# Layer 3 of a four-layer trunk: split q and gate projections, low parts formed on GpSimd, and a new order of norms and gates around the scans

## Chip, core and metric

The kernel runs on one core of a Trainium2 chip. Five engines share that core's work: TensorE (PE; its weight loads are listed apart as PEld), VectorE (DVE), ScalarE (ACT), GpSimd (POOL) and SyncE (SP), which issues most DMAs. Each engine takes its instructions in a fixed order and waits on semaphores for the others. The metric is the device time of one execution in microseconds, the median of several runs.

## What is computed

The reference is a trunk of four layers over 256 latent tokens and 256 context tokens of width 1024, batch 1, all in float32. Layer i takes one mixer and then an MLP. The change touches the mixer of layer 3, a bidirectional gated DeltaNet with 8 key heads and 16 value heads of width 128, in chunks of 64 tokens:

```python
q, k, v = jnp.split(jax.nn.silu(_centred_dwconv(qkv, conv_w)), ...)
q = jnp.repeat(_l2_norm(heads(q)), 2, axis=1) * 128 ** -0.5
k = jnp.repeat(_l2_norm(heads(k)), 2, axis=1)
...
t_inv = lax.linalg.triangular_solve(lmat, eye, lower=True, unit_diagonal=True)
...
def step(s, inp):
    v_new = u_c - w_c @ s
    o = q_c @ s + a_c @ v_new
    s = s * d_c[..., None, None] + jnp.swapaxes(k_c, -1, -2) @ v_new
...
y = (_merge_heads(_rms_norm(o_f + _flip(o_b), norm_g)) * jax.nn.silu(z)) @ w_out
```

z is the gate, another projection of the same input. Layer 3 is the last, so queries, gates and outputs are needed for the latent tokens alone; keys and values are needed for all 512.

## The kernel before

One Python program writes the instructions, and a tile framework orders them on each engine by its own estimate and inserts the semaphores; pools of a fixed number of buffers set how far work may run ahead.

**Projections.** A float32 weight block of 128x1024 is fetched by SP (`raw`), cast on ACT to a high part (`whi`, line 279), and DVE subtracts to get the low part (`wlo`, line 280). `mm3` then makes three products per 128 rows of input (lines 296 to 298: low x high, high x high, high x low). Four raw buffers and four pairs of parts are shared by all blocks; `weights()` keeps two blocks ahead of the one in use. For q and z alone there is another way: `gdn_whole` (line 1542) multiplies the raw float32 block with a float32 copy `u` of the input, eight times 128x256, which the PE runs as two passes each; ACT and DVE have nothing to do for those blocks.

**Products and solves** (`gdn_products`). Keys, queries, values and gates are projected; q, k and v go through a five-tap convolution (`conv`: one ACT scaling and four DVE operations on line 1392, which read PSUM). The value heads are done in two groups of eight. For each group `gdn_solve` makes the decay matrices (lines 1410 to 1421), then runs a loop of 31 steps that inverts 32x32 triangles with two DVE operations a step (lines 1446 and 1448, all operands in SBUF), then joins the blocks by small matmuls (lines 1462 and 1478) and writes the result to DRAM (`uc`, line 1483). Between its steps the jobs of `GDN_JOBS` are started, at the rates of `GDN_PLAN`: a value head (`v`, spilled to DRAM by POOL on line 1591) or a gate head (`z`, spilled on line 1598). POOL otherwise clears buffers and spills the decay matrices (`at`, line 1421).

**Scans** (`gdn_scans`). Four chains c0 to c3, each of eight dependent steps, read the spilled data back. Lanes of jobs are advanced side by side: c0, c1 and the two gate heads that were left; then c2, c3 and a lane with the query norms `n` and the finishing of groups 0 and 1 (`f0`, `f1`); then `f2 f3`. A finish normalises a group's output, gates it, transposes it (line 1718) and multiplies it with four weight blocks `gdn_out` (96 products a group, lines 296 to 298 with `yh` and `yl`), and adds to the residual (line 579).

```python
GDN_LANES = ("c0", "c1", "z"), ("c2", "c3", "n f0 f1"), ("f2 f3",)
GDN_RATES = (1, 1, 0.5), (1, 1, 1.5), (1,)
```

Of the kernel before, what the change touches and what calls it, by code (L numbers as in the profile page):

```python
# [12 lines left out]
F32 = mybir.dt.float32  # L13
# [3 lines left out]
ALU = mybir.AluOpType  # L17
# [4 lines left out]
S = 256  # L22
# [4 lines left out]
KT = D // 128  # L27
# [2 lines left out]
DIFF_AHEAD = 3  # L30
GLA_ROWS = dict(qk=4, la=3, e=9, kb=2, at=1, ob=2)
GLA_STEPS = 2, 1, 1
GDN_LANES = ("c0", "c1", "z"), ("c2", "c3", "n f0 f1"), ("f2 f3",)
GDN_RATES = (1, 1, 0.5), (1, 1, 1.5), (1,)
GDN_ROWS2 = 4, 4, 3, 6, 3, 4
GDN_BANKS = dict(accs=3, st=3, ax=2)
GDN_PLAN = (0, 0.5, 0.4), (0, 0.6, 0.75)
GDN_JOBS = "q0 k1 q1 v v v z z z v v v z z v v z v z v v z z v v z z z z v v z v".split()
TABLES = "natural_log_exp_and_others"
GDN_ROWS = dict(y=3, x=2, v=2, side=3)  # L40
ADA_SUMS = 1
# [116 lines left out]
class Trunk:  # L158
# [100 lines left out]
    def load(self, name, *at):  # L259

        src = self.I[name]
        for j in at:
            src = src[j]
        if name in ("gdn_q", "gdn_z"):
            return self.whole(src)
        last = name == "mla_in" and at[0] in (4, 5) or name in ("mla_out", "diff_out", "gla_out") and at[0] >= 4 or name == "w2" and at[1] >= 4 and at[2] == 3
        return self.halved(self.tail if last else self.wsplit, src)

    def whole(self, src):
        raw = self.wraw.tile([128, 1024], F32, name="raw")  # L270
        self.nc.sync.dma_start(raw[:, :src.shape[-1]], src)
        return raw

    def halved(self, pool, src, n=""):

        nc, width = self.nc, src.shape[-1]
        raw = self.whole(src)
        hi, lo = (pool.tile([128, 1024], F32R, name=m + n) for m in ("whi", "wlo"))
        nc.scalar.copy(hi[:, :width], raw[:, :width])  # L279
        nc.vector.tensor_sub(lo[:, :width], raw[:, :width], hi[:, :width].bitcast(F32))  # L280
        return hi, lo

    def blocks(self):
# [466 lines left out]

    gdn_jobs = GDN_JOBS

# [732 lines left out]
    def gdn_keys(self, grp, key, given=()):  # L1485

        given = list(given)
        n = T2 if key else S
        for j in range(4):
            h = 4 * grp + j  # L1490
            ps = given.pop(0) if given else next(self.proj([("gdn_k", h)])) if key else self.gdn_whole("gdn_q", h)
            y = self.conv(ps, (8 if key else 0) + h, n // S)
            if key:
                self.kT[h] = self.ktp.tile([128, T2], F32, name="kT")
            self.stored(self.silu, self.kT[h] if key else self.qT(h), y, n // S)
            yield
# [42 lines left out]
        self.rsqrt(flat(w), flat(x))  # L1539
        nc.vector.tensor_scalar_mul(self.qnorm, w, -0.5 * 128 ** -0.5)  # L1540

    def gdn_whole(self, name, h):

        w, ps = self.weights(name, h), self.acc()
        for k in range(KT):
            self.nc.tensor.matmul(ps[:, :S], lhsT=w[:, 128 * k:128 * k + 128], rhs=self.u[:, k], start=k == 0, stop=k == KT - 1)  # L1546
        return ps

    def gdn_kk(self, grp):
        nc = self.nc  # L1550
        self.kk = {}
# [40 lines left out]

    def gdn_gate(self, h):
        nc, I = self.nc, self.I
        zp = self.gdn_whole("gdn_z", h)
        sz = self.zs.tile([128, S], F32, name="s")
        self.silu(sz, zp[:, :S])
        nc.gpsimd.dma_start(self.spill[f"z{h // 4}"][:, h % 4], sz)
# [140 lines left out]
    def gdn_open(self, ctx):  # L1739

        nc = self.nc
        pool = self.opener(ctx)
        self.kept, self.ktp = pool("gdn", 1, side="right"), pool("gdnk", 8, side="right")
        side = self.opener(self.uctx)
        self.u = side("gdnu", 1, side="right").tile([128, KT, S], F32, name="u")
        self.zs = side("gdnzs", 2, side="right")
        self.zheads = iter(range(16))
        dram = pool("gdnd", 1, space=bass.MemoryType.DRAM)
        self.gnorm = self.kept.tile([128, 1], F32, name="gnorm")
        nc.vector.tensor_scalar_mul(self.gnorm, self.col("gdn_norm"), -0.5)  # L1750
        self.qnorm = self.kept.tile([128, 2, 8], F32, name="qn")
        self.pick = self.kept.tile([128, 15], F32, name="pick")
        nc.vector.memset(self.pick, 0.0)
        nc.vector.memset(self.pick[:, 7:8], 1.0)
        self.kT, self.o = {}, {}
        self.spill = {"residual": dram.tile([128, KT, S], F32, name="residual")}
        for a in range(4):
            self.spill[f"v{a}"] = dram.tile([128, 4, 4, 128], F32, name=f"v{a}")
            self.spill[f"z{a}"] = dram.tile([128, 4, S], F32, name=f"z{a}")
        for g in range(2):  # L1760
            for p in range(2):
                self.spill[f"uc{g}{p}"] = dram.tile([128, 32, 64], F32, name=f"uc{g}{p}")
                self.spill[f"at{g}{p}"] = dram.tile([128, 2, 512], F32, name=f"at{g}{p}")

    def gdn_products(self):

        nc = self.nc
        with ExitStack() as ctx:
            pool = self.opener(ctx)
            self.open_acc(pool)  # L1770
            rings = {n: pool("gdn" + n, b) for n, b in GDN_ROWS.items()}
            rings["t512"] = self.tmp
            self.rows = lambda n="t512", w=T2: rings[n].tile([128, w], F32, name=n)
            self.srow = lambda: self.rows("side")

            nc.gpsimd.dma_start(self.spill["residual"], self.z[:, :, :S])
            self.lpool, self.x4, self.outer = pool("gdnl", 1), pool("gdnx", 1), pool("gdnt", 1)
            self.once = pool("gdnc", 1)
            self.gdn_tables(self.once)
            first = list(self.proj([("gdn_ba",)] + [("gdn_k", h) for h in range(3)], outer=[64] + [128] * 3))  # L1780
            ba = self.srow()
            self.stored(lambda o, x: nc.scalar.copy(o, x), ba[0:64], first[0][0:64], 2)

            def some(gen, n=None):
                for _ in islice(gen, n):
                    pass

            done, values = set(), iter(range(16))

            def jobs():  # L1790
                for job in self.gdn_jobs:
                    if job[0] in "kq":
                        yield from self.gdn_keys(int(job[1]), job[0] == "k")
                    elif job == "v":
                        yield self.gdn_value(next(values))
                    else:
                        yield self.gdn_gate(next(self.zheads))
                    done.add(job)

            def until(job):  # L1800
                while job not in done:
                    next(main)

            for k in range(KT):
                nc.vector.tensor_tensor(self.u[:, k], *(x[:, k, :S].bitcast(F32) for x in (self.uh, self.ul)), op=ALU.add)
            self.gdn_gates(self.once, self.srow, ba)
            some(self.gdn_keys(0, True, first[1:]))
            main = jobs()
            for grp, n in enumerate(GDN_PLAN):
                until(f"q{grp}")  # L1810
                self.gdn_kk(grp)
                self.gdn_kq(grp)
                if grp == 0:
                    self.gdn_decays(self.kept)
                self.gdn_key_norms(grp)
                due = 0
                for step, _ in enumerate(self.gdn_solve(grp)):
                    due += n[(step >= 8) + (step >= 39)]
                    while due >= 1:
                        some(main, 1)  # L1820
                        due -= 1
            some(main)

    def gdn_scans(self):
        nc = self.nc
        with ExitStack() as ctx:
            pool = self.opener(ctx)
# [27 lines left out]
                            if next(gens[j][0], left) is left:  # L1855
                                left.remove(j)

            def gates():
                for h in self.zheads:
                    self.gdn_gate(h)  # L1860
                    yield

            kinds = dict(z=gates, c=self.gdn_chain, f=self.gdn_finish, n=self.gdn_query_norms)
            lane = lambda jobs: chain.from_iterable(kinds[j[0]](*map(int, j[1:])) for j in jobs.split())
            for n, lanes in enumerate(GDN_LANES):
                if n == 1:
                    self.tables()
                    self.uctx.close()
                    right = lambda *a: pool(*a, side="right")
                    self.zp, self.yp = right("gdnz", 1), right("gdny", 1)  # L1870
                    self.open_ln(right, S)
                    nc.sync.dma_start(self.z[:, :, :S], self.spill["residual"])
                together(*((lane(jobs), rate) for jobs, rate in zip(lanes, GDN_RATES[n])))
            self.ln_finish(*LAT)

# [66 lines left out]
```

## Time and profile before

| what | value |
|---|---|
| median of 3 runs | 2735.97 us (2731.73 to 2740.79) |
| the profiled execution, its own time | 2734.95 us |
| its span, first to last instruction | 2733.2 us |
| busy: PE, DVE, ACT, POOL | 96%, 73%, 46%, 2% of the span |
| mean granted TensorE clock | 0.985 of full speed |

Layer 3's mixer lies between about 2000 and 2520 us of the span; before it are layers 0 to 2, after it the last MLP. A matmul's end is modelled, so a PE that is shown busy is not at its peak; the distance from one start to the next tells what a matmul costs. Idle time of an engine counts only where something else waits for it.

### The profile page before, as it was taken

How to read it: one execution, taken by the hardware profiler on the slowest of the kernel's cores; microseconds unless marked ns; L12 is line 12 of the kernel's file. 1: busy time of each engine (PE TensorE's matmuls, PEld its weight loads, DVE VectorE, ACT ScalarE, POOL GpSimd, SP SyncE). 2: the span in 40 equal slices, each digit the busy share in tenths (PEclk: the TensorE clock that was granted, in tenths of full speed). 3: DMA queues.
4: the chain of work that ended last, by engine and by line, in shares of the span. 5: the costliest groups of instructions: out<-in, count | busy, mean ns of one | idle time of the engine just before them, and what ended most of it. 6: DMA issues, size and time to landing. Idle time of an engine off the chain costs nothing. (4 is left out here: it accounts for less than half of the span.)

```text
span 2733.2 us, 40942 instructions
## 1 busy us (share of the span) xinstructions
PE 2630.0 (96%) x15728; PEld 2137.2 (78%) x15728; DVE 2007.7 (73%) x3796; ACT 1251.6 (46%) x2413; POOL 46.2 (2%) x71
## 2 busy tenths in 40 slices
PE   7999999999999999999999999999999998997998
PEld 5666888888866687888888897888887776667997
DVE  3577898775667798775745489876689996679666
ACT  3555453234556653333445553332464545445544
POOL 0000000000000000000000000000000111000000
PEclk9999999999999999999999999999999998999999
DMA  6533246553221137554221127654323445304453
GB/s 237 169 121 111 68 155 207 185 185 118 65 64 54 47 100 225 191 184 131 73 70 62 55 70 226 195 181 153 104 85 105 160 151 157 90 28 139 155 183 111
DMA packets 125535, 353.25 MB, mean 129 GB/s; under 512 B 37499, under 2 KB 41339, under 8 KB 124828
## 3 DMA queue, kind: packets, MB, share of 16 engines
q1 hardware_dynamic: 121804, 337.00, 38.8%
q0 software_dynamic: 3536, 13.63, 1.4%
q8 instruction: 124, 2.03, 0.3%
q14 instruction: 71, 0.58, 0.1%
HBM read 335.91 MB, written 14.68 MB: 128 GB/s over the span
## 5 line engine op out<-in xcount | busy, mean ns | idle before, releaser
L279 ACT CAST whi<-raw 128x1024 fp32r<-128x1024 f32 (+2 forms) x403 | 410.7, 1024 | 681.6 <-PE acc L297 244.9
L280 DVE TENSOR_TENSOR wlo<-raw,whi 128x1024 fp32r<-128x1024 f32 (+2 forms) x403 | 477.9, 1189 | 209.5 <-ACT whi L279 197.5
L296 PE MATMUL pj<-ul,whi 128*128 128x512 f32 (+1 forms) x1072 | 395.1, 369 | 0.1
L297 PE MATMUL pj<-uh,whi 128*128 128x512 f32 (+1 forms) x1072 | 385.2, 359 | 0.0
L298 PE MATMUL pj<-uh,wlo 128*128 128x512 f32 (+1 forms) x1072 | 383.8, 358 | 0.7 <-DVE wlo L280 0.5
L452 DVE SCALAR_TENSOR_TENSOR acc<-raw,s,acc 128x1024 f32<-128x1024 f32 x252 | 317.2, 1280 | 34.9 <-DMA raw<-in_ada 31.6
L296 PE MATMUL acc<-ul,whi 128*128 128x512 f32 (+3 forms) x888 | 312.5, 352 | 17.6 <-DVE ul L568 10.7
L297 PE MATMUL acc<-uh,whi 128*128 128x512 f32 (+3 forms) x888 | 309.8, 349 | 0.0
L298 PE MATMUL acc<-uh,wlo 128*128 128x512 f32 (+3 forms) x888 | 308.5, 348 | 0.1
L296 PEld LDWEIGHTS pj<-ul,whi 128*128 128x128 f32 x1072 | 204.0, 190 | 36.4 <-issue 6.1
L298 PEld LDWEIGHTS pj<-uh,wlo 128*128 128x128 f32 x1072 | 203.5, 190 | 34.6 <-issue 5.4
L297 PEld LDWEIGHTS pj<-uh,whi 128*128 128x128 f32 x1072 | 203.8, 190 | 29.4 <-issue 5.2
L296 PEld LDWEIGHTS acc<-ul,whi 128*128 128x128 f32 (+2 forms) x888 | 168.6, 190 | 42.3 <-DVE ul L568 12.7
L296 PE MATMUL pj<-hl,whi 128*128 128x512 f32 (+1 forms) x560 | 196.5, 351 | 1.7 <-DVE hl L635 1.3
L297 PE MATMUL acc<-hh,whi 128*128 128x512 f32 (+1 forms) x560 | 195.4, 349 | 0.0
L297 PE MATMUL pj<-hh,whi 128*128 128x512 f32 (+1 forms) x560 | 194.8, 348 | 0.0
L296 PE MATMUL acc<-hl,whi 128*128 128x512 f32 (+1 forms) x560 | 194.8, 348 | 0.0
L298 PE MATMUL acc<-hh,wlo 128*128 128x512 f32 (+1 forms) x560 | 194.7, 348 | 0.0
L298 PE MATMUL pj<-hh,wlo 128*128 128x512 f32 (+1 forms) x560 | 194.2, 347 | 0.0
L298 PEld LDWEIGHTS acc<-uh,wlo 128*128 128x128 f32 (+2 forms) x888 | 168.4, 190 | 21.8 <-issue 1.0
L297 PEld LDWEIGHTS acc<-uh,whi 128*128 128x128 f32 (+2 forms) x888 | 168.5, 190 | 20.9 <-issue 1.2
L634 ACT CAST hh<-t 128x512 fp32r<-128x512 f32 (+1 forms) x128 | 72.2, 567 | 129.7 <-DVE t L633 129.3
(463 smaller groups left out, 4887.2 us busy)
## 6 DMA issues: line engine op xcount, KB each, us to landing
raw<-in_w SPq DMA_DIRECT2D x256, 512.0 KB, 4.2
raw<-in_ada SPq DMA_DIRECT2D x192, 512.0 KB, 4.7
raw<-in_diff_qk SPq DMA_DIRECT2D x16, 512.0 KB, 3.4
raw<-in_gdn_v SPq DMA_DIRECT2D x16, 512.0 KB, 4.0
raw<-in_gdn_z SPq DMA_DIRECT2D x16, 512.0 KB, 4.0
raw<-in_gdn_out SPq DMA_DIRECT2D x16, 512.0 KB, 3.9
raw<-in_mla_in SPq DMA_DIRECT2D x9, 512.0 KB, 7.0
raw<-in_mla_qb SPq DMA_DIRECT2D x12, 384.0 KB, 3.8
```

The lines of the kernel that those rows point to most:

```text
L279: nc.scalar.copy(hi[:, :width], raw[:, :width])
L280: nc.vector.tensor_sub(lo[:, :width], raw[:, :width], hi[:, :width].bitcast(F32))
L296: mm(ps, lhsT=ah, rhs=bl, start=start, stop=False)
L297: mm(ps, lhsT=ah, rhs=bh, start=False, stop=False)
L298: mm(ps, lhsT=al, rhs=bh, start=False, stop=stop)
L452: nc.vector.scalar_tensor_tensor(acc[r], w, self.s[:, k, r:r + 1], acc[r], op0=ALU.mult, op1=ALU.add)
L634: nc.scalar.copy(hh[:, f, :t], r[:, :t])
```

## The change

Gate and query projections become split products like the others, the low parts of the layer's five weights are made by POOL, `u` goes, all sixteen gate heads become jobs of the product stage, the query norms move beside c0 and c1, and `f0 f1` have their lane beside c2 and c3 to themselves. With no gate left in the scans, the pools of the finishes open, and the residual is fetched back, ahead of the first lanes.

```diff
-GDN_LANES = ("c0", "c1", "z"), ("c2", "c3", "n f0 f1"), ("f2 f3",)
-GDN_RATES = (1, 1, 0.5), (1, 1, 1.5), (1,)
+GDN_LANES = ("c0", "c1", "n"), ("c2", "c3", "f0 f1"), ("f2 f3",)
+GDN_RATES = (1, 1, 1), (1, 1, 1.5), (1,)
...
-GDN_JOBS = "q0 k1 q1 v v v z z z v v v z z v v z v z v v z z v v z z z z v v z v".split()
+GDN_JOBS = "q0 k1 q1 v v v z z z v v v z z v v z v z v v z z v v z z z z v v z v z z".split()
+
+LOW_APART = "gdn_k", "gdn_q", "gdn_v", "gdn_z", "gdn_out"
...
-        if name in ("gdn_q", "gdn_z"):
-            return self.whole(src)
...
-        return self.halved(self.tail if last else self.wsplit, src)
+        return self.halved(self.tail if last else self.wsplit, src, low=self.nc.gpsimd if name in LOW_APART else None)
...
-        nc.vector.tensor_sub(lo[:, :width], raw[:, :width], hi[:, :width].bitcast(F32))
+        (low or nc.vector).tensor_sub(lo[:, :width], raw[:, :width], hi[:, :width].bitcast(F32))
...
-            ps = given.pop(0) if given else next(self.proj([("gdn_k", h)])) if key else self.gdn_whole("gdn_q", h)
+            ps = given.pop(0) if given else next(self.proj([("gdn_k", h)])) if key else next(self.proj([("gdn_q", h)], S))
...
-        zp = self.gdn_whole("gdn_z", h)
+        (zp,) = self.proj([("gdn_z", h)], S)
...
-            for k in range(KT):
-                nc.vector.tensor_tensor(self.u[:, k], *(x[:, k, :S].bitcast(F32) for x in (self.uh, self.ul)), op=ALU.add)
...
+            self.tables()
+            self.uctx.close()
+            right = lambda *a: pool(*a, side="right")
+            self.zp, self.yp = right("gdnz", 1), right("gdny", 1)
+            self.open_ln(right, S)
+            nc.sync.dma_start(self.z[:, :, :S], self.spill["residual"])
             for n, lanes in enumerate(GDN_LANES):
-                if n == 1:
-                    self.tables()
-                    self.uctx.close()
...
                 together(*((lane(jobs), rate) for jobs, rate in zip(lanes, GDN_RATES[n])))
```

On DVE, in the loop of the first group's solve, before (`outer` and `xc` are the loop's own tiles, `y` a convolution):

```order
L1448 TENSOR_TENSOR xc<-xc,outer 128x2x26x6
L280 TENSOR_TENSOR wlo<-raw,whi 128x1024
L1446 TENSOR_TENSOR outer<-xb,xc 128x350
L1392 SCALAR_TENSOR_TENSOR y<-acc,cols,y 128x254
L1448 TENSOR_TENSOR xc<-xc,outer 128x2x25x7
```

and at the same place now:

```order
L1448 TENSOR_TENSOR xc<-xc,outer 128x2x26x6
L1392 SCALAR_TENSOR_TENSOR y<-acc,cols,y 128x254
L1446 TENSOR_TENSOR outer<-xb,xc 128x350
L1392 SCALAR_TENSOR_TENSOR y<-acc,cols,y 128x255
L1448 TENSOR_TENSOR xc<-xc,outer 128x2x25x7
```

The subtraction is gone from between the loop's steps; steps and convolutions still take turns.

On POOL, from the decay matrices of the first group on, the order is now (the numbered names are the DRAM tiles of the spills):

```order
L280 TENSOR_TENSOR wlo<-raw,whi 128x1024 x12
L1421 DMA at_17228<-side 128x512 x2
L280 TENSOR_TENSOR wlo<-raw,whi 128x1024
L1421 DMA at_17230<-side 128x512
L280 TENSOR_TENSOR wlo<-raw,whi 128x1024 x2
L1421 DMA at_17230<-side 128x512
L280 TENSOR_TENSOR wlo<-raw,whi 128x1024 x4
L1584 DMA v_17219<-v 512x1x128
L280 TENSOR_TENSOR wlo<-raw,whi 128x1024
L1584 DMA v_17219<-v 512x1x128
L280 TENSOR_TENSOR wlo<-raw,whi 128x1024
L1591 DMA z_17220<-s 128x256
```

Before, this queue held only the spills and the clearings; 64 subtractions now stand between them, 51 of them ahead of the second group's `uc` and 13, of `gdn_out`, behind it.

On PE, in the second pair of chains (`uc` and `kt` are operands of a chain step, `yl` and `yh` the finished output of group 0 on its way into the output projection), now:

```order
L1661 MATMUL st<-t_21621,kt 128x256 x4
L1711 MATMUL ax<-ident,o 128x128 x4
L296 MATMUL acc<-yl,whi 128x256
L297 MATMUL acc<-yh,whi 128x256
L298 MATMUL acc<-yh,wlo 128x256
L296 MATMUL acc<-yl,whi 128x256
L297 MATMUL acc<-yh,whi 128x256
L298 MATMUL acc<-yh,wlo 128x256
L1636 MATMUL acc<-S,kT 64x256 x4
```

In PE's order 155 of the 384 output products now stand ahead of the last chain matmul and 229 behind it; before, it was 30 and 354.

## Rows read from the trace of the kernel before

**Rows 1.** Busy time by stretch: products, first chains, second chains, finishes behind them.
```profile
core 0: us, PE busy (x) PEld busy (x) DVE busy (x) ACT busy (x) POOL busy (x), PEclk, DMA share, GB/s
2000.00:2285.00 285.00, 262.70 (x2255) 212.95 (x2255) 263.55 (x460) 151.91 (x303) 40.37 (x58) 0.96 0.42 133
2285.00:2372.00 87.00, 84.22 (x560) 56.86 (x555) 52.26 (x179) 33.67 (x100) 1.63 (x3) 0.97 0.42 122
2372.00:2463.00 91.00, 83.20 (x553) 54.85 (x553) 58.61 (x209) 39.76 (x143) 0.00 (x0) 0.96 0.13 37
2463.00:2520.00 57.00, 48.54 (x371) 45.85 (x369) 52.17 (x142) 29.68 (x77) 0.00 (x0) 0.97 0.42 131
```

**Rows 2.** Groups of DVE, 2000 to 2285 us: count, busy us, mean ns, idle before.
```profile
L1392 DVE SCALAR_TENSOR_TENSOR y<-pj,cols,y 128x508 f32<-128x508 f32 (+3 forms) x64 | 43.6, 681 | 2.1 <-ACT y L1389 1.9
L1448 DVE TENSOR_TENSOR xc<-xc,outer 128x62 f32<-128x62 f32 (+15 forms) x62 | 32.8, 528 | 0.9
L1446 DVE TENSOR_TENSOR outer<-xb,xc 128x62 f32<-128x62 f32 (+15 forms) x62 | 32.7, 528 | 0.8
L280 DVE TENSOR_TENSOR wlo<-raw,whi 128x1024 fp32r<-128x1024 f32 x24 | 29.4, 1224 | 4.4 <-ACT whi L279 4.4
L1410 DVE TENSOR_TENSOR side<-mask,gx 128x512 f32<-128x512 f32 x16 | 11.0, 684 | 0.4 <-DMA at<-side 0.4
```

**Rows 3.** Line 1805, the sum that makes u: durations min/median/max, first and last start.
```profile
L1805 DVE TENSOR_TENSOR u<-uh,ul x8: 417/419/424, 1986.7 to 1993.4; 128x256 f32<-128x256 f32 x8
```

**Rows 4.** Order of time, PE: start, us, instruction, count; a whole q head, what follows.
```profile
2018.13 3.69 PE L1546 MATMUL acc<-u,raw 128*128 128x256 f32 x16 [2.03 <-issue]
2021.76 0.33 PE L1557 MATMUL st<-kT 128*64 128x64 f32 x2
```

**Rows 5.** Order of time, PE, in the last MLP: split products of 256 columns.
```profile
2560.00 0.28 PE L296 MATMUL acc<-hl,whi 128*128 128x256 f32 x1
2560.12 0.28 PE L297 MATMUL acc<-hh,whi 128*128 128x256 f32 x1
2560.24 0.28 PE L298 MATMUL acc<-hh,wlo 128*128 128x256 f32 x1
```

**Rows 6.** Groups of ACT, 2000 to 2285 us: the cast to the high part.
```profile
L279 ACT CAST whi<-raw 128x1024 fp32r<-128x1024 f32 x25 | 26.2, 1051 | 33.2 <-DMA raw<-in_gdn_v 21.0 <-DMA raw<-in_gdn_k 7.7 <-DMA raw<-in_gdn_out 2.4
```

**Rows 7.** Groups of POOL, whole span: the clearings.
```profile
L1472 POOL MEMSET xc<- 32x1024 f32 x4 | 4.7, 1173 | 18.2 <-DVE xa L1453 18.1
L1431 POOL MEMSET xc<- 128x2048 f32 x2 | 3.6, 1813 | 635.5 <-PE pj L298 634.0 <-DMA uc<-xc 1.5
```

**Rows 8.** Order of time, DVE beside POOL, behind the second group's loop.
```profile
2270.81 2.38 POOL L1472 MEMSET xc<- 32x1024 f32 x2 [6.88 <-DVE xa L1453]
2271.26 1.04 DVE L1471 COPY xc<-xd 32x1024 f32<-32x1024 f32 x1
2273.11 0.69 DVE L1471 COPY xc<-xd 32x1024 f32<-32x1024 f32 x1
2276.49 1.51 DVE L1471 COPY xa<-xd 32x1024 f32<-32x1024 f32 x1 [1.91 <-PE st L1462]
2276.51 2.38 POOL L1472 MEMSET xa<- 32x1024 f32 x2 [3.31 <-PE st L1462]
2277.49 1.40 POOL L1472 MEMSET xa<- 32x1024 f32 x1
2278.84 3.23 POOL L1839 MEMSET at<- 64x512 f32 x5
2279.94 1.23 DVE L280 TENSOR_TENSOR wlo<-raw,whi 128x1024 fp32r<-128x1024 f32 x1
```

**Rows 9.** Waits of POOL, 2000 to 2290 us: total, times, longest us.
```profile
POOL v L1591 <- ACT v L1590: 93.9, 11, 35.1
POOL at L1421 <- DVE side L1420: 77.9, 4, 64.8
POOL xc L1472 <- DVE xa L1453: 18.1, 2, 11.3
```

**Rows 10.** Groups of PE beside the chains: gates (2285 to 2372 us), query norms (2372 to 2463).
```profile
L1546 PE MATMUL acc<-u,raw 128*128 128x256 f32 x32 | 9.0, 399 | 0.0
L1529 PE MATMUL st<-t,pick 128*8 128x256 f32 x16 | 4.5, 380 | 0.0
```

**Rows 11.** Groups of PE and of DVE in the finishes, 2463 to 2520 us.
```profile
L296 PE MATMUL acc<-yl,whi 128*128 128x256 f32 x115 | 34.0, 296 | 3.2 <-DVE z L579 2.3 <-DVE yl L654 0.8
...
L280 DVE TENSOR_TENSOR wlo<-raw,whi 128x1024 fp32r<-128x1024 f32 x13 | 15.8, 1219 | 0.6 <-ACT whi L279 0.4
```

More of the change, by code (lines that the diff above doesn't have):

```diff
@@ L272, in whole, with halved @@
         return raw
-    def halved(self, pool, src, n=""):
+    def halved(self, pool, src, n="", low=None):
         nc, width = self.nc, src.shape[-1]
@@ L1540, in gdn_query_norms @@
         nc.vector.tensor_scalar_mul(self.qnorm, w, -0.5 * 128 ** -0.5)
-    def gdn_whole(self, name, h):
-        w, ps = self.weights(name, h), self.acc()
-        for k in range(KT):
-            self.nc.tensor.matmul(ps[:, :S], lhsT=w[:, 128 * k:128 * k + 128], rhs=self.u[:, k], start=k == 0, stop=k == KT - 1)
-        return ps
     def gdn_kk(self, grp):
@@ L1744, in gdn_open @@
         side = self.opener(self.uctx)
-        self.u = side("gdnu", 1, side="right").tile([128, KT, S], F32, name="u")
         self.zs = side("gdnzs", 2, side="right")
@@ L1802, in until @@
                     next(main)
-            for k in range(KT):
-                nc.vector.tensor_tensor(self.u[:, k], *(x[:, k, :S].bitcast(F32) for x in (self.uh, self.ul)), op=ALU.add)
             self.gdn_gates(self.once, self.srow, ba)
@@ L1856, in together @@
                                 left.remove(j)
[L1858 to L1863, printed above, removed]
-            lane = lambda jobs: chain.from_iterable(kinds[j[0]](*map(int, j[1:])) for j in jobs.split())
-            for n, lanes in enumerate(GDN_LANES):
-                if n == 1:
-                    self.tables()
-                    self.uctx.close()
[L1869 to L1872, printed above, removed]
+            kinds = dict(c=self.gdn_chain, f=self.gdn_finish, n=self.gdn_query_norms)
+            lane = lambda jobs: chain.from_iterable(kinds[j[0]](*map(int, j[1:])) for j in jobs.split())
+            self.tables()
[4 more added lines that the diff above has]
+            nc.sync.dma_start(self.z[:, :, :S], self.spill["residual"])
+            for n, lanes in enumerate(GDN_LANES):
                 together(*((lane(jobs), rate) for jobs, rate in zip(lanes, GDN_RATES[n])))
```

## The prediction

> **What bounds the kernel now.** I read busy time by stretch first, since layer 3 is four stretches with different limits [rows 1]. In the products and solves (285 us) DVE is busy 263.6 us and PE 262.7; a PE end is modelled, so the engine to believe is DVE, with 21.4 us idle. In the two pairs of chains (87 and 91 us) DVE is busy 52 and 59 us and PE 84 and 83: each step waits for the one before, and no engine is full. In the finishes behind the chains (57 us) DVE is busy 52 us, PE 48.5. Next I read DVE's groups in the products [rows 2]: 24 subtractions that make low parts take 29.4 us, the two operations of the solve's loop 65.5 us, the convolutions some 87 us (the row shown and an equal one for the other PSUM pool). Then come POOL's groups and waits [rows 7, 9] for what its queue is like, and the order of time where DVE and POOL meet [rows 8]. All sums are made against the profiled execution's own 2735 us (1.8 us over its span); it lies 1 us under the median of the runs shown.
>
> **Products and solves, part by part.**
>
> *DVE loses* the 24 subtractions, 29.4 us [rows 2], and the eight sums that make u, 8 x 0.42 = 3.4 us [rows 3], which lie just ahead of this stretch where DVE is as full.
>
> *PE.* A q or z head takes 3.6 us as raw float32 (2018.13 to 2021.76) [rows 4]. Split, it is 24 products at 0.12 us from start to start [rows 5], 2.9 us. 22 heads lie in this stretch now, 79 us; the change puts 24 there, 69 us. These 10 us count only if DVE ceases to be the bound; here I cost them at nothing.
>
> *ACT* gains 24 casts of 1.05 us [rows 6], 25 us on 152 busy of 285 [rows 1]. The idle half hides them; without that cover they would stand in line ahead of ACT's scaling of the convolutions, at most 25 us.
>
> *POOL* gains 64 subtractions; 48 of them (8 k less the first three, 8 q, 16 v, 16 z, three of `gdn_out`) run in this stretch. No row shows POOL subtracting. Its clearings give bounds: 2048 elements take 1.81 us [rows 7], so one stream of 1024 takes 0.9 us, the low end, and three streams (two read, one written) in turn 2.7 us, the high end. A subtraction must at least read twice, 1.8 us; I take 2.25, midway between that and the high end. 48 x 2.25 = 108 us of 285: POOL is far from full.
>
> *DVE against POOL.* This is the disputed price. A DVE copy of 32x1024 takes 0.69 us by itself and 1.04 and 1.51 us where POOL is clearing a buffer. The slow one of 1.51 us started with the first of two clearings, and the 0.82 us that it lost end about where that clearing does, since the second is on from 2277.49; the second in turn takes 1.40 us, where the first had 0.98 [rows 8]. So whoever came second stood until the other's instruction was over. A subtraction on DVE beside POOL's clearings took 1.23 us, its usual time [rows 8, 2]. What happens when POOL itself reads two operands while DVE reads two is not in this trace. Bounds: 0, as that subtraction had it, and the whole 2.25 us per POOL subtraction, as the copies had it. I take the copies' side, because a POOL instruction that reads and writes is more like the case in which they met than one that only writes is. Some 36 of the 48 fall into the decay matrices and the loops, where DVE's work with two SBUF operands comes one convolution apart at most: DVE does one of these (0.68 us) and then stands, 2.25 - 0.68 = 1.6 us each, 58 us. The other 12 meet the convolutions of keys and queries, four in a row, 0.4 us each: 5 us. DVE then has 263.6 - 29.4 + 63 = 297 us; half of its present idle time, waits for ACT and PE, goes under the new ones, 11 us stay: 308 against 285, +23. With the sums gone (-3.4), +20.
>
> [...]
>
> *POOL's queue* runs in order. Its clearings behind a solve's loop wait up to 11.3 us for the loop's last results [rows 9], and the `uc` spills stand behind them. Two or three low parts are now queued behind that at the hand-over from the first group to the second, while two value blocks lie ready in front of PE. Between nothing and 11 us; I take 5. Weights on SP: no DMA is added, but the fetch of the residual moves ahead of eight gate and value blocks; it needs z's columns, which the second group's decay matrices are the last to read, long before: 0.
>
> Products: **+25 us**.
>
> **Scans, part by part.**
>
> *First chains.* Two gate heads go, 32 passes, 9.0 us busy; the norms come, 16 passes, 4.5 us [rows 10]. Chains leave gaps that hide most of both: between 0 and -5, I take -3.
>
> *Second chains.* 125 more output products stand among them (155 for 30): 125 x 0.12 = 15 us of PE [rows 5]; what they bring for DVE fits its 32 idle us [rows 1]. PE is shown idle 7.8 us there, and the norms leave 4.5 [rows 1, 10], so 12 us fit at best: +3; at worst nothing does, +15. Queued behind each output product on PE is a chain step, so not all gaps will be hit: +8.
>
> *Finishes behind.* 345 products, three times the 115 of one kind [rows 11], take 57 us, 0.165 each. 125 fewer are 20.6 us, and DVE loses 13 subtractions, 15.8 us [rows 11], that were part of that pace. Low end -28 (229 at PE's own 0.12), high end -12; I take -19.
>
> Scans: **-14 us**. Sum: 2735 + 25 - 14 = **2746 us**.
>
> **The rivals.**
>
> 1. *DVE and POOL don't meet.* If DVE runs beside POOL's subtractions as it did beside the clearing in [rows 8], the stretch loses up to 33 us of DVE; PE, 10 us lighter, is then as full, and I take -22 of the products, nothing for the queue, and -15 for the scans: 2735 - 37 = 2698. For it: the one two-operand DVE operation that met POOL lost nothing. Against: that POOL work did not read. It decides from about 0.7 us of standing per subtraction downward, where 48 of them just spend the 33 us.
>
> 2. *POOL's queue starves PE.* The spills wait on POOL for 93.9 us in 11 waits and 77.9 us in 4 [rows 9], and each low part behind such a spill is late. If 20 of the 48 come 1.5 us too late for PE on top of the forecast, 2746 + 30 = 2776. Against: two blocks are always ahead, and the long waits were of an empty queue.
>
> 3. *The second chains don't take the finishes in.* The order has 155 products there, but if each pushes the chain back, the gain behind is given back: scans 0, 2735 + 25 = 2760. PE's 83 of 91 us [rows 1] speaks for it, the modelled ends against.
>
> **How the numbers follow.** A measurement of this kernel can tell about 0.3%, 8 us, from no change. Forecast 0.48, by itself from 2728 to 2765 (standing between 1.1 and 1.9 us, scans between -6 and -22): slower 0.29, same 0.17, faster 0.02. Rival 1 0.36: faster 0.34, same 0.02. Rival 2 0.08: slower. Rival 3 0.08: slower 0.06, same 0.02. Together slower 0.43, same 0.21, faster 0.36. The range runs from the middle of rival 1, less 8 us for its own spread, 2690, to 2772, which leaves out about a tenth at each end.
>
> **What would show it.** In the profile of the changed kernel: the two operations on lines 1446 and 1448 with a mean of 0.8 us or more instead of 0.53 while the convolutions keep 0.68 (forecast), or unchanged (rival 1); the distance between POOL's subtractions where it has several in a row, 2.25 us or not; PE idle before `wlo` on line 298 released by POOL (rival 2); the products' stretch at 313, 263 or 343 us; the second chains at 94 to 106 us, and no more than 40 us from their end to the last output product. Wrong altogether would be a POOL subtraction near 0.9 us or over 4, or a DVE that stands beside POOL in the scans, where its operations read PSUM.

## The result, and the profile after

The changed kernel takes **2803.42 us** (median of 3 runs, 2800.89 to 2805.23) against 2735.97: 67 us more, a ratio of 1.0245 with a 95% interval of 1.0215 to 1.0275. The forecast was 2746 with a range of 2690 to 2772: the sign was right, the size was not, and the time lies outside the range.

To compare stages I cut both profiled executions at the same instructions: the first DVE operation of layer 3's mixer (line 1301), the chains' first product with `t` (`ax<-t,uc`), the last `ax<-t,at` of the first and of the second pair, and the last product that reads `yh`. Busy time by stretch of the kernel before, then of the changed one (columns as in [rows 1]): products, first chains, second chains, finishes.

```profile
1986.10:2296.90 310.80, 286.12 (x2421) 232.64 (x2419) 279.43 (x504) 170.05 (x347) 42.07 (x62) 0.96 0.41 133
2296.90:2370.30 73.40, 71.85 (x477) 48.16 (x477) 48.77 (x173) 25.18 (x77) 1.09 (x2) 1.00 0.38 107
2370.30:2461.90 91.60, 83.45 (x554) 54.87 (x553) 58.95 (x209) 39.77 (x141) 0.00 (x0) 0.96 0.14 36
2461.90:2518.80 56.90, 49.64 (x380) 46.95 (x379) 51.33 (x139) 29.06 (x79) 0.00 (x0) 0.97 0.44 138
```

```profile
1977.30:2355.20 377.90, 302.92 (x2641) 252.23 (x2640) 323.50 (x472) 193.72 (x373) 165.39 (x113) 0.87 0.36 114
2355.20:2428.40 73.20, 68.62 (x462) 42.86 (x462) 48.10 (x171) 25.99 (x84) 0.00 (x0) 1.00 0.31 85
2428.40:2537.00 108.60, 98.40 (x673) 70.87 (x672) 68.19 (x244) 46.11 (x157) 14.20 (x6) 0.97 0.22 64
2537.00:2585.30 48.30, 35.80 (x247) 33.15 (x246) 40.55 (x92) 19.57 (x55) 14.15 (x6) 0.86 0.27 88
```

Products +67.1 us (forecast +25), first chains -0.2 (-3), second chains +17.0 (+8), finishes -8.6 (-19): 75.3 in layer 3. Layer 3 began 8.8 us earlier in the second profile. Ahead of it the change touches only the low parts of three key blocks at the end of layer 2, and in the five experiments that leave those on DVE the start lies anywhere from 1976 to 1984, so I don't count the 8.8 us as the change's.

In the products DVE's busy time grew by 44.1 us (279.4 to 323.5), *and* its idle time by 23.0 (31.4 to 54.4). PE is busy 302.9 of 377.9, at a granted clock of 0.87 instead of 0.96. The groups of DVE that answer to [rows 2], 2000 to 2342.6 us:

```profile
L1448 DVE TENSOR_TENSOR xc<-xc,outer 128x62 f32<-128x62 f32 (+15 forms) x62 | 55.7, 899 | 1.0
L1446 DVE TENSOR_TENSOR outer<-xb,xc 128x62 f32<-128x62 f32 (+15 forms) x62 | 49.3, 795 | 1.1
L1392 DVE SCALAR_TENSOR_TENSOR y<-pj,cols,y 128x508 f32<-128x508 f32 (+3 forms) x64 | 42.8, 671 | 2.7 <-ACT y L1389 2.4
...
L1410 DVE TENSOR_TENSOR side<-mask,gx 128x512 f32<-128x512 f32 x16 | 14.1, 883 | 2.5 <-DMA at<-side 2.5
```

Operations with both inputs in SBUF grew (the loop's two from 0.53 to 0.90 and 0.80 us, line 1410 from 0.68 to 0.88); the convolution, which reads PSUM, did not (0.68 to 0.67). That was the sign I had named. POOL's group in the same stretch, and one meeting in the order of time:

```profile
L280 POOL TENSOR_TENSOR wlo<-raw,whi 128x1024 fp32r<-128x1024 f32 x48 | 119.5, 2496 | 114.4 <-ACT whi L279 95.1 <-PE pj L298 18.8 <-issue 0.2
```

```profile
2143.39 0.64 DVE L1448 TENSOR_TENSOR xc<-xc,outer 128x462 f32<-128x462 f32 x1
...
2143.99 2.39 POOL L280 TENSOR_TENSOR wlo<-raw,whi 128x1024 fp32r<-128x1024 f32 x1 [3.93 <-ACT whi L279]
...
2144.07 2.79 DVE L1446 TENSOR_TENSOR outer<-xb,xc 128x440 f32<-128x440 f32 x1
...
2147.44 0.60 DVE L1448 TENSOR_TENSOR xc<-xc,outer 128x440 f32<-128x440 f32 x1
```

A POOL subtraction takes 2.39 us at its median (the mean of 2.50 holds some longer ones). The DVE operation of about 0.6 us that came 0.08 us behind it ended at 2146.86, about its own time behind POOL's end at 2146.38.

What DVE's standing did to the others shows in the waits of PE and ACT, 2000 to 2342.6 us (total, times, longest):

```profile
PE ax L1580 <- ACT x L235: 33.3, 10, 6.8
PE acc L296 <- DVE y L1392: 16.2, 5, 6.3
PE st L1413 <- DVE side L1410: 13.4, 7, 4.3
ACT x L235 <- DVE y L1392: 34.4, 9, 6.8
```

Before, PE waited 2.8 us for that `x` (ACT's gate on a convolved block, ahead of its transpose); the last line shows ACT waiting in turn for the convolution on DVE. No wait of PE for `wlo` is listed: POOL's queue starved nobody (rival 2). In the finishes small operations of DVE stand as well (2537 to 2585.3 us):

```profile
L654 DVE TENSOR_TENSOR yl<-t,yh 128x256 fp32r<-128x256 f32 x8 | 5.0, 621 | 0.3 <-ACT yh L653 0.2
L543 DVE SCALAR_TENSOR_TENSOR t<-ss,t 128x8 f32<-128x8 f32 x2 | 3.9, 1970 | 1.3 <-ACT t L542 1.3
L1698 DVE TENSOR_TENSOR ss<-ss,qn 128x8 f32<-128x8 f32 x4 | 2.7, 667 | 0.1
```

Line 543 took 0.16 us before, line 654 0.42.

### The profile page after: what moved, and what is told of

Its sections match the earlier page's. It is cut to its first block, busy times and chain, and to the rows that moved or that the text cites. A ratio compares the mean times of both kernels' runs of the same rounds, so it can differ in the third digit from the quotient of the medians.

```text
span 2799.1 us, 41427 instructions
## 1 busy us (share of the span) xinstructions
PE 2636.6 (94%) x15920; PEld 2148.7 (77%) x15920; DVE 2050.9 (73%) x3748; ACT 1274.0 (46%) x2437; POOL 204.9 (7%) x135
## 5 line engine op out<-in xcount | busy, mean ns | idle before, releaser
L279 ACT CAST whi<-raw 128x1024 fp32r<-128x1024 f32 (+2 forms) x427 | 435.9, 1026 | 718.1 <-PE pj L297 254.1
L280 DVE TENSOR_TENSOR wlo<-raw,whi 128x1024 fp32r<-128x1024 f32 (+1 forms) x363 | 429.2, 1186 | 201.0 <-ACT whi L279 189.8
L296 PE MATMUL pj<-ul,whi 128*128 128x512 f32 (+1 forms) x1168 | 423.0, 362 | 0.7 <-DVE y L1392 0.6
L297 PE MATMUL pj<-uh,whi 128*128 128x512 f32 (+1 forms) x1168 | 414.1, 355 | 0.0
L298 PE MATMUL pj<-uh,wlo 128*128 128x512 f32 (+1 forms) x1168 | 412.3, 353 | 0.4 <-DVE wlo L280 0.2
L296 PE MATMUL acc<-ul,whi 128*128 128x512 f32 (+3 forms) x984 | 346.3, 352 | 32.1 <-DVE y L1392 16.2
L298 PE MATMUL acc<-uh,wlo 128*128 128x512 f32 (+3 forms) x984 | 343.0, 349 | 1.2 <-DVE wlo L280 1.2
L297 PE MATMUL acc<-uh,whi 128*128 128x512 f32 (+3 forms) x984 | 343.0, 349 | 0.0
L280 POOL TENSOR_TENSOR wlo<-raw,whi 128x1024 fp32r<-128x1024 f32 x64 | 158.3, 2479 | 916.5 <-DVE z L579 599.5
L298 PEld LDWEIGHTS acc<-uh,wlo 128*128 128x128 f32 (+2 forms) x984 | 191.6, 195 | 24.5 <-DVE wlo L280 2.0
```

The lines of the kernel that those rows point to most:

```text
L280: (low or nc.vector).tensor_sub(lo[:, :width], raw[:, :width], hi[:, :width].bitcast(F32))
L296: mm(ps, lhsT=ah, rhs=bl, start=start, stop=False)
L297: mm(ps, lhsT=ah, rhs=bh, start=False, stop=False)
L298: mm(ps, lhsT=al, rhs=bh, start=False, stop=stop)
```

## Experiments

Medians, and the stretches of each profile cut as above (us):

| run | median | products | 1st chains | 2nd chains | finishes |
|---|---|---|---|---|---|
| before | 2736.0 | 310.8 | 73.4 | 91.6 | 56.9 |
| changed kernel | 2803.4 | 377.9 | 73.2 | 108.6 | 48.3 |
| low_dve | 2765.9 | 345.5 | 72.0 | 110.2 | 39.3 |
| lanes_raw | 2740.3 | 312.2 | 71.8 | 109.7 | 39.3 |
| sub_twice | 2924.0 | 472.2 | 73.3 | 108.5 | 61.3 |
| clear_first | 2827.4 | 392.3 | 71.9 | 108.9 | 58.1 |
| quarters | 2789.1 | 359.1 | 73.3 | 110.8 | 47.4 |
| eighths | 2783.9 | 361.7 | 71.9 | 108.8 | 43.4 |
| raw_kvout | 2771.8 | 343.6 | 71.9 | 112.3 | 53.1 |
| raw_kvout_q | 2769.3 | 341.2 | 71.9 | 109.1 | 47.0 |
| kq_pool | 2768.3 | 351.6 | 72.1 | 110.2 | 38.6 |
| vz_pool | 2786.5 | 370.9 | 72.0 | 111.9 | 39.9 |
| out_pool | 2773.7 | 351.2 | 72.8 | 108.4 | 48.4 |
| dve_twice | 2766.5 | 341.3 | 73.5 | 91.8 | 56.9 |

The kernel before ran beside each of the three groups of four with medians of 2738.8, 2736.9 and 2736.4. Each stretch comes from one profiled execution. For lanes_raw and dve_twice that one lies 11 us under the run's median (2729.6 and 2755.9), so between these two and the others the stretches are good to some 10 us and the medians are to be preferred.

### The change taken apart

**low_dve**, the low parts back on DVE:

```diff
-LOW_APART = "gdn_k", "gdn_q", "gdn_v", "gdn_z", "gdn_out"
+LOW_APART = ()
```

> The changed kernel with all low parts back on DVE; the split q and z products and the new lanes stay. Theory (DVE stands beside POOL's subtractions): the two loop operations go back to 0.53 us each, DVE loses about 71 us of standing in the products and takes 48 subtractions of 1.22 us, 59 us, back, and its idle time falls from 43 us to about the 22 of before: products about 33 us shorter, the finishes some 8 us longer, 2778 us in all (2760 to 2790). Rival (the standing is harmless; the split q and z products, their casts and the new lanes cost the time): DVE has 59 us more and nothing back, 2840 us or more.

Measured: 2765.88 (ratio to before 1.0097, 1.0072 to 1.0122). 37.5 us of the 67 are POOL's. DVE's row in the products:

```profile
1983.50:2329.00 345.50, 300.97 (x2647) 252.58 (x2646) 302.75 (x521) 192.29 (x374) 43.66 (x64) 0.87 0.40 130
```

Its 302.8 us hold 49 subtractions of 59.4 us in all. Each overlaps its neighbours on DVE a little, so without them DVE would be busy 249.5 us, not 243.4. The changed kernel has 323.5 without one: 74 us of standing, 1.5 us a subtraction (the expectation of quarters still counts 80). The expectation erred on the idle time: it is 42.7 us here, not 22, with no POOL subtraction anywhere.

**lanes_raw**, the scans' part alone (with `GDN_LANES`, `GDN_RATES` and `GDN_JOBS` of the change, on the kernel before; q and z raw, all low parts on DVE):

```diff
+            self.tables()
+            self.uctx.close()
...
+            nc.sync.dma_start(self.z[:, :, :S], self.spill["residual"])
             for n, lanes in enumerate(GDN_LANES):
-                if n == 1:
...
```

> The kernel before with only the scans' part of the change: the new lanes and rates, all sixteen gates as jobs of the products, the pools of the finishes opened ahead of the lanes; q and z stay raw float32 products and the low parts stay on DVE. My own term for the scans: -14 us, with up to 4 us for the two gates more in the products, 2721 to 2727 us. Rival (the second pair of chains is pushed back by as much as the finishes behind it gain): 2733 to 2742 us.

Measured: 2740.31, ratio 1.0008 (0.9995 to 1.0021): the rival. Its second chains:

```profile
2364.80:2474.50 109.70, 99.15 (x669) 70.93 (x669) 74.61 (x250) 46.60 (x160) 0.00 (x0) 0.94 0.21 62
```

The finishes gain 17.6 us, as forecast (19). The second chains lose 18.1: PE's busy time grows by 15.7, the full 125 x 0.12 us, and its idle time (8.2 us before, 10.6 now) takes in nothing.

The three parts of the change are thus: lanes 1.5 us (by the ratio 2), split q and z products with their low parts on DVE 25.6 (2740.3 to 2765.9), the low parts to POOL 37.5. The split brings DVE 24 subtractions and ACT 24 casts; no run tells what each of these costs.

### The price of a POOL subtraction

**sub_twice** and **clear_first**, a second subtraction, or three clearings ahead, for each low part:

```diff
-        (low or nc.vector).tensor_sub(lo[:, :width], raw[:, :width], hi[:, :width].bitcast(F32))
+        for _ in range(2 if low else 1):
+            (low or nc.vector).tensor_sub(lo[:, :width], raw[:, :width], hi[:, :width].bitcast(F32))
```

```diff
+        for _ in range(3 if low else 0):
+            low.memset(lo[:, :width].bitcast(F32), 0.0)
         (low or nc.vector).tensor_sub(lo[:, :width], raw[:, :width], hi[:, :width].bitcast(F32))
```

> The changed kernel with each of POOL's 64 subtractions done twice, the second over the same tiles. Theory (each makes DVE stand about 1.5 us): 48 more in the products, 70 us, and some 9 us in the scans, about 2880 us (2850 to 2900). Rival (a low part is only late, POOL's queue is what costs): POOL has over half of the products' stretch free, so at most 20 us more, 2803 to 2823 us.

> The changed kernel with three POOL clearings of the low part's tile (128x1024, about 0.9 us each) ahead of each POOL subtraction: 2.7 us more of POOL writing SBUF, none of it reading. If DVE stands only beside a POOL instruction that reads SBUF: 0 to 12 us more (some low parts later), 2803 to 2815 us. If any POOL access to SBUF makes DVE stand: as with the doubled subtraction, 2860 to 2890 us.

Measured: 2923.98, 120.6 more, and 2827.42, 24.0 more. 49 more subtractions lengthen the products by 94.3 us, 1.92 each, and DVE's busy time by 86.1 (323.5 to 409.6), 1.76 each: more than I had put down, and far from the rival's 20. As many microseconds of POOL work that only writes (142 us of clearings in the products, against 121 of second subtractions) cost a fifth of that, between my two cases for it. Here DVE's busy time in the products grew by 21.5 us (323.5 to 345.0) and the stretch by only 14.4: 7 us went under DVE's idle time. How DVE met one row of clearings:

```profile
2080.74 0.68 DVE L1412 TENSOR_TENSOR side<-mask,gx 128x512 f32<-128x512 f32 x1
...
2080.96 3.40 POOL L281 MEMSET wlo<- 128x1024 f32 x3 [2.90 <-PE acc L300]
...
2081.34 0.68 DVE L1419 TENSOR_TENSOR xb<-side,z 128x512 f32<-128x512 f32 x1
...
2082.05 1.41 DVE L1438 COPY xa<-xd 32x1024 f32<-32x1024 f32 x1
2083.50 0.69 DVE L1422 TENSOR_TENSOR side<-side,z 128x512 f32<-128x512 f32 x1
```

The two-input operations lost nothing beside these clearings (0.68 us each), the copy did (1.41 for 0.69; the mean of these four is 2.69). The 24 us are thus no pure queueing: copies stand too. Beside a subtraction another one-input operation stood as well: line 1326 took 1.56 us in the changed kernel and 0.16 in the one before. Why the copy stood beside work that only writes, and the two-input operations did not, no run shows.

**quarters** and **eighths**, the subtraction in pieces:

```diff
+        for c in range(0, width, 256 if low else width):
+            c = slice(c, c + 256 if low else width)
+            (low or nc.vector).tensor_sub(lo[:, c], raw[:, c], hi[:, c].bitcast(F32))
```

> The changed kernel with each POOL subtraction done in four pieces of 128x256, about 0.6 us each. Theory (whoever comes second stands until the instruction under way is over): DVE then stands 0.6 us at most, and the convolution of 0.68 us between two loop operations hides a piece; of the 80 us of standing in the products 20 to 30 are left, 2750 us (2735 to 2775). Rival (the two engines share one port, and the sum of what they want from it stays): no gain, 2790 to 2810 us.

> The same in eight pieces of 128x128. Theory: as with four or a little better for DVE, but POOL's fixed cost per piece makes low parts later, 2740 to 2775 us. Rival: 2790 to 2820 us.

Measured: 2789.12 and 2783.93, 14 and 19 us less than the changed kernel, against 30 to 65 expected; nearer to the rival in time, though the shared port that it supposes no run shows. Eighths bring DVE's busy time in the products to 290.4 us, 33 less, but its idle time rises from 54.4 to 71.3. And the pieces didn't let DVE in reliably; of **quarters**:

```profile
2118.25 1.51 POOL L282 TENSOR_TENSOR wlo<-raw,whi 128x256 fp32r<-128x256 f32 x2
2118.86 4.88 DVE L1448 TENSOR_TENSOR outer<-xb,xc 128x510 f32<-128x510 f32 x1
2119.63 0.62 POOL L1593 DMA_DIRECT2D z<-s  x1
...
2120.22 2.82 POOL L282 TENSOR_TENSOR wlo<-raw,whi 128x256 fp32r<-128x256 f32 x4
```

One DVE operation of 0.7 us stood through two pieces, a DMA issue and four more pieces, and ended 0.7 us behind the last.

### Which subtractions

**kq_pool**, **vz_pool** and **out_pool** put the low parts of some weights alone on POOL, as in

```diff
-LOW_APART = "gdn_k", "gdn_q", "gdn_v", "gdn_z", "gdn_out"
+LOW_APART = "gdn_v", "gdn_z"
```

> The changed kernel with the low parts of keys and queries alone on POOL (16), the others on DVE. Beside the run with all on DVE (2766 us): if these 16 meet convolutions, which read PSUM, as my prediction had it (0.4 us of standing against 1.22 saved): 13 less, 2753 us. If they cost what the others do (about 1.9 us each): 11 more, 2777 us.

> The changed kernel with the low parts of values and gates alone on POOL (32). They fall into the decay matrices and the loops, where DVE works from SBUF: at 1.9 us each against 1.22 saved, 22 to 27 more than 2766, 2788 to 2793 us. At the prediction's 1.6 us with half of DVE's idle time swallowed: 2766 us or less.

> The changed kernel with the low parts of the output weights alone on POOL (16, three of them in the products). In the changed kernel the finishes behind the chains are 9 us longer than with these on DVE and the second chains about 2 shorter: 2766 + 7 + 2 = 2775 us. If those 9 us come from elsewhere: 2760 to 2766 us.

Measured: 2768.27, 2786.53 and 2773.68, that is +2.4, +20.6 and +7.8 on low_dve, 31 of the 37.5 us. Values and gates are the expensive ones (0.65 us each beyond the 1.22 they save DVE). Keys and queries gain nothing, where I had 13 us: beside the convolutions DVE works through the decay gates and the key norms there, and in the changed kernel line 1336 stands at a mean of 0.74 us for 0.28, line 1508 at 0.76 for 0.42. In kq_pool DVE stands some 12 us for the 13 subtractions that lie in the products, 0.9 each. The 16 of the output cost 9 us in the finishes and give back 1.8 in the second chains.

**raw_kvout** has the lanes of lanes_raw, q and z raw, and only k, v and out on POOL; **raw_kvout_q** the same in four pieces:

```diff
+LOW_APART = "gdn_k", "gdn_v", "gdn_out"
...
-        return self.halved(self.tail if last else self.wsplit, src)
+        return self.halved(self.tail if last else self.wsplit, src, low=self.nc.gpsimd if name in LOW_APART else None)
```

> The kernel before with the new lanes (as in the run lanes_raw, 2740 us), q and z raw float32 products, and the low parts of k, v and out on POOL: 24 subtractions in the products and 13 in the scans. If a POOL subtraction costs the products what the changed kernel and the doubled subtraction show (about 1.9 us against 1.22 of DVE's own): +16, and +9 in the finishes, 2765 us (2755 to 2775). At the price of my prediction (1.3 us, and half of DVE's idle time swallowed): 2740 us or less, plus 9.

> The same with each POOL subtraction in four pieces of 128x256. If pieces cut the standing to a quarter to a third: DVE loses 29 us and stands 12 to 15, and PE, 289 us busy of 312, sets the stretch: 2725 to 2745 us. If the port's time is shared whatever the pieces: as the run with whole subtractions, 2755 to 2775 us.

Measured: 2771.77, at the price of the earlier runs, and 2769.27, so pieces change little here either. The sum of DVE's work explains neither. Products of lanes_raw, raw_kvout, raw_kvout_q:

```profile
1980.80:2293.00 312.20, 288.99 (x2455) 233.85 (x2453) 278.89 (x504) 172.30 (x351) 43.21 (x64) 0.98 0.42 137
```

```profile
1979.00:2322.60 343.60, 305.78 (x2454) 245.00 (x2452) 282.35 (x479) 170.87 (x350) 104.65 (x89) 0.92 0.39 125
```

```profile
1980.90:2322.10 341.20, 302.00 (x2454) 242.33 (x2453) 270.70 (x479) 170.81 (x350) 124.20 (x164) 0.93 0.40 126
```

The last has 8 us *less* DVE work than lanes_raw and is 29 longer (as are the medians). PE is busy 13 us more with the same matmuls, at a granted clock of 0.93 for 0.98 (17 us in raw_kvout, at 0.92), and its idle time grows by 16 (14.6). Where that is lost, one place shows; PE, order of time, raw_kvout, behind the second loop:

```profile
2280.35 1.12 PE L1588 MATMUL ax<-ident,x 128*128 128x128 f32 x4 [11.81 <-ACT x L234]
...
2283.84 0.63 PE L298 MATMUL pj<-uh,whi 128*128 128x512 f32 x1
2284.26 0.63 PE L299 MATMUL pj<-uh,wlo 128*128 128x512 f32 x1
```

PE stood 11.8 us at a transpose whose convolution was late on DVE, with a value head queued behind it; then that head's products started 0.42 to 0.43 us apart, up to 2287.68, and 0.22 to 0.24 apart from 2288.88 on. In the changed kernel products of this shape start 0.43 us apart where the granted clock was 0.50 (2099.0 to 2104.6 us), and 0.23 apart where it was 1.00 (2105 to 2110).

**dve_twice** tests the step about idle time without POOL, on the kernel before:

```diff
-        nc.vector.tensor_sub(lo[:, :width], raw[:, :width], hi[:, :width].bitcast(F32))
+        for _ in range(times):
+            nc.vector.tensor_sub(lo[:, :width], raw[:, :width], hi[:, :width].bitcast(F32))
```

(`times` is 2 for keys and values.)

> The kernel before with the low parts of keys and values made twice, both times on DVE: 24 subtractions of 1.22 us more, 29 us, 21 of them behind the first products, and POOL as before. My step, that half of DVE's idle time (11 us) takes such an addition in: 2737 + 18 = 2755 us. If PE and DVE are both so full that whatever is added to one comes on top: 2765 to 2772 us, with DVE's idle time as before or more.

Measured: 2766.49, ratio 1.0099 (1.0071 to 1.0126), 30 us for 29 added.

```profile
1977.10:2318.40 341.30, 296.68 (x2420) 238.30 (x2419) 300.93 (x525) 168.10 (x346) 41.45 (x62) 0.91 0.38 123
```

By the medians the addition costs its full length. In the profile the products are 30.5 us longer, with 21 more subtractions there (26 us by their own time, 21.5 of DVE's busy time, since they overlap their neighbours); DVE's idle time went from 31.4 to 40.4 and PE's clock from 0.96 to 0.91. Here idle time took in nothing.

No version beat the kernel before; lanes_raw equals it.

## Why the prediction was right in sign and wrong in size

*The mechanism and its price* held. A POOL subtraction took 2.39 us (2.25 taken, a midpoint between two bounds), and DVE stood at least until it was over (to 2146.86 for 2146.38 in the meeting above), in the loops (0.80 and 0.90 us for 0.53), in the decay matrices (0.88 for 0.68 on line 1410) and not in the convolutions (0.67 for 0.68). The standing came to 74 us instead of 63. The loops and matrices gave 52 of my 58 (39.5 in the loop's two lines); the other subtractions, costed at 5 for meeting convolutions only, gave the rest, and kq_pool has 12 for keys and queries alone. The 25 subtractions that left DVE freed 27 us of its busy time, not 29, as each overlaps its neighbours. Together that is 14 us of the 42 by which the products missed.

**The step that failed** is the one behind it: "half of its present idle time, waits for ACT and PE, goes under the new ones, 11 us stay". Instead of shrinking by 10.7 us DVE's idle time grew by 23.0: a miss of 34 (the 5 us for the queue, not seen as such, come off the sum). dve_twice shows that it did not hold without POOL either: 29 us of plain DVE work cost 30. My own first paragraph had the numbers: PE and DVE were both some 92% busy, and I took DVE alone for the bound because PE's ends are modelled. What made DVE late left PE at a transpose or a convolution's buffer (33.3 and 16.2 us of waits), the granted clock of the stretch was 0.87 for 0.96, and DVE then waited for PE. Behind two of PE's waits for a convolution, of 3.74 and 6.34 us, the clock was 0.50 (2088.3 to 2090.9 and 2099.0 to 2104.6 us), and 1.00 behind that (2091.2 to 2092.5 and 2105 to 2110). That the waits bring the clock down is my reading of this order; no run shows it by itself, and the 20 us below have a clock of 0.66 with PE idle for 0.24. The wait that grew most lies behind the first group's loop. DVE stood 12 us for a key product (through ACT's copy `z`); before, 0.2. The rows are that wait before, then the same wait and its stretch of 20 us in the changed kernel:

```profile
2167.95 0.43 DVE L1508 TENSOR_TENSOR side<-z,eye 128x256 f32<-128x256 f32 x1 [0.23 <-ACT z L1559]
2194.03 0.43 DVE L1508 TENSOR_TENSOR side<-z,eye 128x256 f32<-128x256 f32 x1 [12.05 <-ACT z L1552]
2177.30:2197.30 20.00, 19.76 (x479) 15.92 (x473) 7.61 (x9) 13.59 (x22) 9.93 (x8) 0.66 0.33 129
```

PE was busy 19.8 of those 20 us at a clock of 0.66, and DVE 7.6. I let the idle time of one engine absorb a delay that the other engine could not make up; the forecast and the rivals built on it (2 and 3) had the same flaw, so the range was short above. The step is not wrong everywhere: clear_first added 21.5 us of DVE's busy time for 14.4 of the stretch, from a kernel that already had 54 us of idle time.

*PE* losing 10 us by the split was rightly counted as no gain; in low_dve PE is busy 12 us more than in lanes_raw, at 0.87 against 0.98, though by [rows 4, 5] the 24 split heads should take it 17 us less. *ACT*'s casts stayed hidden as far as the waits show: ACT is busy 193.7 of 377.9, and where PE waited for ACT's gate, ACT waited for DVE (34.4 us). *The queue's 5 us* can't be told apart from the rest; rival 2 did not happen. Rival 1 is excluded by the loop's two lines and by sub_twice.

*Scans*, -14 forecast, +8 measured, -1 in lanes_raw. The finishes' term was right as long as DVE is alone (-17.6); with POOL beside it 9 us are given back (out_pool: 48.4 against 39.3), on operations on lines 543, 654 and 1698 with all inputs in SBUF. I had written that a DVE standing in the scans would be "wrong altogether, where its operations read PSUM": the chains' do, the finishes' don't all. The second chains' term was mis-sized: "12 us fit at best" for 15 added, and none fitted, +18; this is rival 3, which I had given 0.08. (The low end for the finishes, 229 products at 0.12, is -30 and not -28; nothing hangs on it.)

What stays open is how the 23 us of DVE's idle time divide between PE's clock and the fixed order of the queues. 12 us are the wait shown above, where both act, and 5 are a longer wait for PE at the end of the stretch (14.0 for 8.8), most of which lanes_raw has too (12.8). Each experiment moved both causes, and holding one still was not tried.

## What to carry to other kernels

Here two engines were some 92% and 90% busy (PE 286.1 and DVE 279.4 of 310.8 us) and fed each other through a few buffers, and work added to one cost its full length (30 us for 29 in dve_twice). In such a case start from that price, and don't count on idle time to absorb it. POOL work that read two operands from SBUF made DVE stand 1.5 to 1.8 us on average of its 2.39 and cost the stretch 1.9 (sub_twice), for a subtraction that took DVE 1.22 itself. DVE's convolutions, which read PSUM, lost nothing beside it (0.68 us before, 0.67 in the changed kernel); before moving work there, check what else runs beside it (keys and queries gained nothing).

## What was not expected of the hardware

A DVE operation that waited for POOL was not always served when POOL's instruction ended: POOL's next ones went first. The longest case among whole, single subtractions is in vz_pool (in sub_twice one operation stood 12.88 us through five of them):

```profile
2244.44 4.74 POOL L280 TENSOR_TENSOR wlo<-raw,whi 128x1024 fp32r<-128x1024 f32 x2
2244.90 7.50 DVE L1446 TENSOR_TENSOR outer<-xb,xc 128x312 f32<-128x312 f32 x1
...
2249.07 0.60 POOL L1591 DMA_DIRECT2D z<-s  x1
2249.65 2.40 POOL L280 TENSOR_TENSOR wlo<-raw,whi 128x1024 fp32r<-128x1024 f32 x1
2252.32 0.73 DVE L1392 SCALAR_TENSOR_TENSOR y<-acc,cols,y 128x508 f32<-128x508 f32 x1
```

Two subtractions, a DMA issue of 0.60 us and a third subtraction passed while one operation of 0.47 us stood for 7.50. This goes with the small gain of the short pieces, which came in direct succession: 14 and 19 us of the 37.5.
